# RWKV layer: scores split around the head norms, bonus product on GpSimd, decays and norms set between projections

## The chip, the core and the metric

The program runs on one core of one Trainium2 chip. A core has TensorE (matrix products, PE in the rows), VectorE (DVE), ScalarE (ACT), GpSimd (POOL) and queues of DMAs, each with an instruction stream of its own that is worked off in order; semaphores tie them together. The metric is the time of one execution on the device in microseconds (us), lower being better, given as the median of several runs.

## The reference

The program computes a long stack of layers for 256 tokens of width 1024. The change touches one of them, the RWKV mixer of the second block's layer 1 (16 heads of 64), cut here to what matters:

```python
def rwkv7_mixer(x, mu, w_rkv, w0, w1, w2, a0, a1, a2, g1, g2, k_k, k_a, r_k, ln_g, ln_b, w_out):
    mix = lambda i: x + xx * mu[i]                      # xx: the token before minus this one
    r, k, v = ((mix(i) @ w_rkv[i]).astype(F32) for i in range(3))
    w_log = -jax.nn.softplus(-(w0 + jnp.tanh(mix(3) @ w1) @ w2)) - 0.5
    decay = jnp.exp(-jnp.exp(w_log))
    a = jax.nn.sigmoid(a0 + (mix(4) @ a1) @ a2)
    g = jax.nn.sigmoid(mix(5) @ g1) @ g2
    kk = heads(k * k_k); kk = kk / jnp.maximum(norm_of_head(kk), 1e-12)
    k = k * (1.0 + (a - 1.0) * k_a)
    def step(S, xt):                                    # over the tokens
        r_t, w_t, k_t, v_t, a_t, b_t = xt
        sa = jnp.einsum('bhij,bhj->bhi', S, a_t)
        S = S * w_t[:, :, None, :] + sa[..., :, None] * b_t[..., None, :] + v_t[..., :, None] * k_t[..., None, :]
        return S, jnp.einsum('bhij,bhj->bhi', S, r_t)
    ...
    bonus = (jnp.sum(rh * kh * r_k, axis=-1, keepdims=True) * vh).reshape(B, T, D)
    return ((y + bonus) * g).astype(x.dtype) @ w_out
```

## The kernel before

The kernel does the recurrence in four chunks of 64 tokens. Features lie on the partitions in eight blocks j of 128 (two heads each). A float32 product of the projections is done as three passes of split operands (`hi*hi`, `lo*hi`, `hi*lo`); ScalarE makes `hi`, VectorE makes `lo`. TensorE's order is the order of the code (`manual_schedule`); the other engines' orders come from a scheduler and are fixed when the program is built. What a tile waits for follows from its buffers: a pool tag with n buffers lets the (n+1)-th tile begin only when an earlier one has been read for the last time. PSUM has four banks for products (tag `ps`, two rings of two) and two for accumulators (tag `acc`).

The stages, with the lines of the code before:

- **decays** (L1625 to L1630): for each block two products of 64 rows by 256 columns, `pl2`, and a Sigmoid on ScalarE into `P1`.
- **project** (L1634): a quarter of the key or receptance projection: two accumulations of 24 products into `prk`, each copied by ScalarE into `P2`. The order is key 0, key 1, receptance 0, key 2, receptance 1, key 3, receptance 2, receptance 3.
- **inverse_norms(half)** (L1663): ScalarE squares four key blocks (`kk2`, two buffers of tag `m`, shared with the running sum `cum`), TensorE sums them by head into `pss`, ScalarE takes the root, VectorE the maximum and the reciprocal: `inv`.
- **spread(half)** (L1677): four products of 16 rows spread `inv` over the features: `pk`.
- **phase(j)** (L1688): the running sum of the decays, its exponentials (`E1`, `e3`), the key `km`, the normed key `kk`, the bonus product `f` = receptance * `r_k` * key (L1703, four buffers), and then, in place over `P1` and `P2`, the four decayed operands (L1708 to L1711). L1710 and L1711 overwrite receptance and key of the block. Two `W` buffers (`e4`) serve all phases.
- **turn(j)** (L1716): two products of `f` with the head selector into `pbon` (L1719), and the transposes of block j (L1723), copied by ScalarE into `BKt`.
- **scores(jg)** (L1729): for each of four chunks eight products of 64 rows into two banks `pA`; VectorE masks them into `AM` (L1741), ScalarE copies the diagonal blocks into `Dg` (L1745). `scores(0)` covers the heads of blocks 0 to 3, `scores(1)` those of 4 to 7.
- **the solve** (L1810 to L1839): VectorE transposes `Dg`, does 31 pairs of small steps and transposes back to `Xc` and `Zc`. TensorE meanwhile works on the value projection (`project_v`, four parts) and `products(0)`, then `merge_y` needs `Xc`, `merge_z` needs the copies `Ys`.
- **gates(t, hh)** (L1893): a product into an `acc` bank and five VectorE steps. The recurrence behind it (`middle`, L1929) begins with a product `pU` into the bank that `gates(1, 0)` leaves.

## Time and profile before

| | us |
|---|---|
| median of 3 runs | 2569.16 |
| lowest and highest | 2565.10, 2569.85 |
| the profiled execution, its time | 2571.75 |
| the profiled execution, its span | 2570.0 |
| PE busy | 2448.4 (95%) |
| DVE busy | 1443.1 (56%) |
| ACT busy | 1169.4 (46%) |
| POOL busy | 141.6 (6%) |

The profile is one execution; its time is its span and 1.75 us around it. Times in rows count from the span's start. The RWKV mixer lies between about 1062 and 1280; the change touches 1081 to 1216. A row of the timeline gives the start, the time from the first start to the last end, engine, line, operation, tiles, the count, and in brackets the idle time before it with what ended that. A float32 product shows as two records on PE, a `prk` pass as one.

### The profile page before, as it was taken

The page shows a single profiled execution, that of the slowest core. Times are in us where ns is not written, and L with a number is a line of the kernel's source. Part 1 is how long each engine was busy: PE and PEld are TensorE (multiplying, and loading weights), DVE is VectorE, ACT ScalarE, POOL GpSimd, SP SyncE. Part 2 cuts the span into 40 slices and gives each one's busy share as a digit, 9 for nine tenths or more (in the row PEclk, how much of TensorE's full clock was granted, in tenths as well). Part 3 has the DMA queues.
Part 4 walks back from the last instruction along what each step waited for, and adds up shares of the span by engine and source line. Part 5 has one row for each costly group of instructions (what it writes and reads, how often), then busy time and mean ns, then how long its engine had stood idle before and what let it go on. Part 6 is the DMA issues. An engine that isn't in the chain of part 4 may idle for free.

```text
span 2570.0 us, 42656 instructions
## 1 busy us (share of the span) xinstructions
PE 2448.4 (95%) x17989; PEld 2199.1 (86%) x17989; DVE 1443.1 (56%) x2194; ACT 1169.4 (46%) x1904; POOL 141.6 (6%) x241
## 2 busy tenths in 40 slices
PE   8987679999999999999899999999999999999998
PEld 7764349999899999887799999989999999998998
DVE  7831145558655555588855554565465465477543
ACT  5411134447544544564544444443454454476442
POOL 0100000001200000000000000011100000003000
PEclk9988989999999999999999999999999999999999
DMA  8599996555465565432355565555455555554551
GB/s 280 182 385 419 390 339 212 197 167 177 146 212 181 165 212 180 133 106 90 129 201 179 171 208 182 174 198 166 162 195 183 181 197 181 167 182 164 181 182 64
DMA packets 326016, 502.27 MB, mean 195 GB/s; under 512 B 24833, under 2 KB 278969, under 8 KB 314297
## 3 DMA queue, kind: packets, MB, share of 16 engines
q1 hardware_dynamic: 317616, 481.28, 54.3%
q10 hardware_dynamic: 8200, 18.19, 2.1%
q8 instruction: 143, 2.34, 0.4%
q14 instruction: 57, 0.46, 0.1%
HBM read 498.38 MB, written 1.05 MB: 194 GB/s over the span
## 4 chain that ended last, share of the span: by engine, by line
PE 67%; issue 10%; DVE 6%; ACT 2%; POOL 2%; DMA 2%; ACTq 0%; DVEq 0%; SPq 0%; POOLq 0%
PE gu L362 28%; PE acc L383 18%; PE gut L371 4%; PE pv L371 3%; PE prk L362 2%; PE pu L362 2%; PE pqk L362 2%; PE pg L371 2%; DVE lo L236 1%; PE po L371 1%; DMA wx<-in_w_down_dram 1%; ACT junk L269 1%; POOL rs_r L271 1%; PE pt L304 1%; DVE xn L299 1%
## 5 line engine op out<-in xcount | busy, mean ns | idle before, releaser
L236 DVE TENSOR_TENSOR lo<-raw,hi 128x1024 fp32r<-128x1024 f32 x714 | 851.6, 1217 | 462.1 <-ACT hi L235 462.0
L235 ACT ACTIVATE hi<-raw 128x1024 fp32r<-128x1024 f32 x714 | 723.3, 1045 | 388.1 <-PE acc L383 218.4
L362 PE MATMUL gu<-xh,lo 128*128 128x256 f32 x2304 | 324.0, 284 | 0.0
L362 PE MATMUL gu<-xh,hi 128*128 128x256 f32 x2304 | 323.4, 283 | 0.0
L362 PE MATMUL gu<-xl,hi 128*128 128x256 f32 x2304 | 322.9, 283 | 0.0
L362 PEld LDWEIGHTS gu<-xh,hi 128*128 128x128 f32 x2304 | 300.9, 189 | 5.8
L362 PEld LDWEIGHTS gu<-xl,hi 128*128 128x128 f32 x2304 | 296.7, 189 | 0.0
L362 PEld LDWEIGHTS gu<-xh,lo 128*128 128x128 f32 x2304 | 295.7, 189 | 0.0
L383 PE MATMUL acc<-lo,hh 128*128 128x512 f32 x704 | 224.5, 397 | 0.0
L383 PE MATMUL acc<-hi,hl 128*128 128x512 f32 x704 | 221.6, 394 | 0.0
L383 PE MATMUL acc<-hi,hh 128*128 128x512 f32 x704 | 220.9, 395 | 0.0
L423 ACT ACTIVATE sg<-gu 128x256 f32<-128x256 f32 x144 | 55.3, 384 | 339.8 <-PE gu L362 339.8
L425 DVE TENSOR_TENSOR hm<-sg,gu 128x256 f32<-128x256 f32 x144 | 60.2, 418 | 199.8 <-ACT sg L423 199.8
L383 PEld LDWEIGHTS acc<-lo,hh 128*128 128x128 f32 x704 | 132.8, 189 | 30.6
L383 PEld LDWEIGHTS acc<-hi,hl 128*128 128x128 f32 x704 | 132.2, 188 | 30.2
L383 PEld LDWEIGHTS acc<-hi,hh 128*128 128x128 f32 x704 | 127.2, 188 | 23.7
L270 POOL TENSOR_SCALAR rs_a<-ms 128x1 f32<-128x1 f32 x46 | 19.6, 426 | 1659.3 <-ACT junk L269 1637.9
L1027 PE MATMUL pgu<-wx,xg 128*32 128x256 f32 x816 | 77.9, 430 | 22.5 <-DMA wx<-in_w_gate_dram 14.2
L1027 PEld LDWEIGHTS pgu<-wx,xg 128*32 128x32 f32 x816 | 35.8, 123 | 54.8 <-DMA wx<-in_w_gate_dram 20.2
L236 DVE TENSOR_TENSOR hl<-hm,hh 128x256 fp32r<-128x256 f32 x144 | 60.7, 422 | 35.3 <-ACT hh L235 35.3
L371 PE MATMUL gut<-hi,xh 128*128 128x256 f32 x512 | 78.3, 291 | 0.0
L371 PE MATMUL gut<-lo,xh 128*128 128x256 f32 x512 | 75.1, 287 | 1.6 <-DVE lo L236 1.5
(523 smaller groups left out, 3299.4 us busy)
## 6 DMA issues: line engine op xcount, KB each, us to landing
raw<-in_ffn_w_gu_dram SPq DMA_DIRECT2D x176, 1024.0 KB, 5.1
raw<-in_ffn_w_down_dram SPq DMA_DIRECT2D x88, 1024.0 KB, 4.8
wx<-in_w_gate_dram SPq DMA_DIRECT2D x24, 1024.0 KB, 19.9
wx<-in_w_up_dram SPq DMA_DIRECT2D x24, 1024.0 KB, 19.9
raw<-in_ml_w_in_dram SPq DMA_DIRECT2D x24, 1024.0 KB, 5.2
raw<-in_rt_w_in_dram SPq DMA_DIRECT2D x24, 1024.0 KB, 5.3
wx<-in_w_down_dram SPq DMA_DIRECT2D x22, 1024.0 KB, 11.3
row<-in_norm_g_dram ACTq DMA_DIRECT2D x24, 512.0 KB, 4.2
```

The costliest lines, as they stand in the source:

```text
L235: return (self.nc.scalar.activation(out=hi, in_=src, func=AF.Copy), self.nc.vector.tensor_tensor(out=lo, in0=src, in1=hi.bitcast(F32), op= ...
L236: self.nc.vector.tensor_tensor(out=lo, in0=src, in1=hi.bitcast(F32), op=OP.subtract))
L269: nc.scalar.activation(out=junk[:, qs], in_=src[:, qs], func=AF.Square, scale=mul ** 0.5 / 32.0, accum_out=ms[:, q:q + 1])
L271: nc.gpsimd.tensor_tensor(out=r, in0=a, in1=self.half[:, 0:1], op=OP.pow)
L299: last = nc.vector.scalar_tensor_tensor(out=xn[:, qs], in0=x[:, qs], scalar=rs, in1=g[:, qs], op0=OP.mult, op1=OP.mult)
L304: nc.tensor.transpose(out=pt[:, i, :], in_=xn[:, 128 * k:128 * k + 128], identity=self.c("ident"))
L362: nc.tensor.matmul(out=out, lhsT=a[:, k, c0:c0 + m], rhs=b[:, :, k, :], start=(n == 0), stop=(n == 3 * KD - 1))
L371: nc.tensor.matmul(out=out, lhsT=b[:, t, k, :], rhs=a[:, k, :], start=(n == 0), stop=(n == 3 * KD - 1))
L383: self.down_ins.append(nc.tensor.matmul(out=acc[t][:, n, :], lhsT=s[:, t, :], rhs=r[:, q, 512 * n:512 * n + 512], start=(first and q == 0 ...
L423: nc.scalar.activation(out=sg, in_=gu[:, 0, :], func=AF.Silu)
L425: nc.vector.tensor_tensor(out=hm, in0=sg, in1=gu[:, 1, :], op=OP.mult)
L1027: nc.tensor.matmul(out=p[32 * e:32 * e + 32, 256 * i:256 * i + 256], lhsT=xg[q // 2][:, k, 4 * (q % 2) + e, :], rhs=part(w[e], k, KD), sta ...
```

## The change

1. Of the 16 decays, four stay in front; the other twelve stand one by one behind the passes of `project(xk, kT, 0)` and `project(xk, kT, 1)` (`between`).
2. `inverse_norms(0)` stands inside `project(xr, rT, 0)`, behind its first half.
3. The bonus product is a GpSimd product without `r_k`; `r_k` goes into the selector (`hsr`, one small VectorE product made once).
4. `scores(0)` moves in front of `project(xr, rT, 2)`: chunks 0 and 1 ahead of `inverse_norms(1)`, chunks 2 and 3 behind it; `spread(1)` follows at once, ahead of the projection that stood between. `rwmask` has a buffer of its own.
5. `turn` 0 to 5 stand behind `project(xr, rT, 3)`, ahead of `scores(1)`; 6 and 7 stay behind `project_v(0)`.
6. `project_v(3)` stands whole in front of `merge_y`; behind it come `products(1)`, `merge_z(0)`, `gates(0, 0)`, `merge_z(1)` and the other gates.

```diff
--- before.py
+++ after.py
@@ -1622,20 +1622,32 @@
         P2 = [mp.tile([128, 4, 2, S], F32, name=f"P2{i}", tag=f"P2{i}") for i in range(2)]
         kT = lambda j: P2[j // 4][:, j % 4, 0, :]
         rT = lambda j: P2[j // 4][:, j % 4, 1, :]
-        for j in range(KD):
-            for i, b in enumerate(("w0", "a0")):
-                r = slice(64 * i, 64 * i + 64)
-                p = self.ps.tile([128, S], F32, name="pl2", tag="ps")
-                nc.tensor.matmul(out=p, lhsT=l2[r, 128 * j:128 * j + 128], rhs=hwa[r], start=True, stop=True)
-                nc.scalar.activation(out=P1[:, j, i, :], in_=p, func=AF.Sigmoid, bias=self.col(b, j))
+        def decays():
+            for j in range(KD):
+                for i, b in enumerate(("w0", "a0")):
+                    r = slice(64 * i, 64 * i + 64)
+                    p = self.ps.tile([128, S], F32, name="pl2", tag="ps")
+                    nc.tensor.matmul(out=p, lhsT=l2[r, 128 * j:128 * j + 128], rhs=hwa[r], start=True, stop=True)
+                    nc.scalar.activation(out=P1[:, j, i, :], in_=p, func=AF.Sigmoid, bias=self.col(b, j))
+                    yield
+        decay = decays()
+        for _ in range(4):
+            next(decay)
         xr = self.xt()
         mix_split(0, xr)
-        def project(x, dst, c):
+        def project(x, dst, c, between=None):
             w = self.take()
             for q in range(2):
                 p = self.ps.tile([128, S], F32, name="prk", tag="ps")
-                self.mm_t(p, w, 128 * q, x)
+                for n, (a, b) in enumerate(((w[0], x[0]), (w[1], x[0]), (w[0], x[1]))):
+                    for k in range(KD):
+                        nc.tensor.matmul(out=p, lhsT=a[:, k, 128 * q:128 * q + 128], rhs=b[:, :, k, :],
+                                         start=(n == 0 and k == 0), stop=(n == 2 and k == KD - 1))
+                    if between:
+                        between(3 * q + n)
                 nc.scalar.activation(out=dst(2 * c + q), in_=p, func=AF.Copy)
         self.load_const("headsel", "headsel_t", "segment", "blockodd", pool=mp)
@@ -1646,6 +1658,11 @@
         oka = mp.tile([128, KD], F32, name="oka")
         nc.vector.tensor_scalar(out=oka, in0=ka_t[:, ka0:ka0 + KD], scalar1=-1.0, scalar2=1.0, op0=OP.mult, op1=OP.add)
         WL = mp.tile([128, KD, 4], F32, name="WL")
+        rk_t, rk0 = self.cols["r_k"]
+        hsr = mp.tile([128, KD, 2], F32, name="hsr")
+        nc.vector.tensor_tensor(out=hsr, in0=hs[:, 14:16].unsqueeze(1).to_broadcast([128, KD, 2]),
+                                in1=rk_t[:, rk0:rk0 + KD].unsqueeze(2).to_broadcast([128, KD, 2]), op=OP.mult)
         PU = lambda c: slice(0, 64) if c % 2 else slice(64, 128)
@@ -1700,7 +1717,7 @@
             nc.gpsimd.tensor_copy(out=WL[:, j, :], in_=E1[:, :, 64])
             nc.vector.scalar_tensor_tensor(out=kk, in0=k, scalar=self.col("k_k", j), in1=pk.pop(j), op0=OP.mult, op1=OP.mult)
             nc.vector.tensor_tensor(out=km, in0=km, in1=k, op=OP.mult)
-            nc.vector.scalar_tensor_tensor(out=f, in0=r, scalar=self.col("r_k", j), in1=km, op0=OP.mult, op1=OP.mult)
+            nc.gpsimd.tensor_tensor(out=f, in0=r, in1=km, op=OP.mult)
             nc.vector.scalar_tensor_tensor(out=g, in0=kk, scalar=-1.0, in1=a, op0=OP.mult, op1=OP.mult)
             ar, bk = P1[:, j], P2[j // 4][:, j % 4]
             Ev = E1.rearrange("p (e o) t -> p e o t", o=2)
@@ -1716,7 +1733,7 @@
         def turn(j):
             f = fs.pop(j)
             for t in range(NT):
-                nc.tensor.matmul(out=pb[:, t, 2 * j:2 * j + 2], lhsT=f[:, 128 * t:128 * t + 128], rhs=hs[:, 14:16],
+                nc.tensor.matmul(out=pb[:, t, 2 * j:2 * j + 2], lhsT=f[:, 128 * t:128 * t + 128], rhs=hsr[:, j, :],
                                  start=True, stop=True)
             pt = self.ps.tile([128, 4, 128], F32, name="pbt", tag="ps")
             for c in range(4):
@@ -1726,10 +1743,10 @@
         AM, UV = [], []
-        def scores(jg):
-            for c in range(4):
+        def scores(jg, cs=range(4)):
+            for c in cs:
                 pA = [self.ps.tile([128, 4, 128], F32, name="pA", tag="ps") for _ in range(2)]
                 for i in range(4):
                     for a in range(2):
@@ -1762,10 +1779,9 @@
             for _ in steps:
                 pass
-        project(xk, kT, 0)
-        project(xk, kT, 1)
-        inverse_norms(0)
-        project(xr, rT, 0)
+        project(xk, kT, 0, lambda i: next(decay))
+        project(xk, kT, 1, lambda i: next(decay))
+        project(xr, rT, 0, lambda i: inverse_norms(0) if i == 2 else None)
         spread(0)
         project(xk, kT, 2)
         phase(0)
@@ -1777,33 +1793,32 @@
         for k in range(KD):
             mix(xv[:, k, :], 2, k)
         BKt.extend([big("t1", "BKt", shape=(128, 2, KD, 128)), big("t2", "BKt", shape=(128, 2, KD, 128))])
+        self.load_const("rwmask", pool=mp)
+        rwm = self.c("rwmask")
+        Dg = mp.tile([128, 32, 32], F32, name="Dg")
         project(xk, kT, 3)
+        AM.extend([slot(c % 2, "AM", [128, NH, 128]) for c in range(4)])
+        scores(0, (0, 1))
         inverse_norms(1)
+        scores(0, (2, 3))
         self.ahead = 1
-        project(xr, rT, 2)
         spread(1)
         pb = self.pa.tile([128, NT, 16], F32, name="pbon", tag="acc")
-        turn(0)
-        turn(1)
+        project(xr, rT, 2)
         phase(4)
         phase(5)
         project(xr, rT, 3)
-        turn(2)
-        turn(3)
         phase(6)
         phase(7)
-        self.load_const("rwmask", pool=mp, tag="hwa")
-        rwm = self.c("rwmask")
-        AM.extend([slot(c % 2, "AM", [128, NH, 128]) for c in range(4)])
-        Dg = mp.tile([128, 32, 32], F32, name="Dg")
-        scores(0)
+        for j in range(6):
+            turn(j)
         SV = mp.tile([128, 2, 32, 32], F32, name="SV", tag="P20")
         E = SV[:, 1]
         UV.extend([slot(t, "UV", [128, 2, NH, 64]) for t in range(NT)])
         scores(1)
         every(project_v(0))
-        for j in range(4, 8):
+        for j in range(6, 8):
             turn(j)
         bon = mp.tile([128, NT, 16], F32, name="bon")
         nc.vector.tensor_copy(out=bon, in_=pb)
@@ -1873,16 +1888,13 @@
                     nc.scalar.activation(out=Tt[r, us, 1, :], in_=p[r], func=AF.Copy)
         g2 = self.take()
-        v3 = project_v(3)
-        for _ in range(2): next(v3)
+        every(project_v(3))
         copied = [merge_y(t) for t in range(NT)][0]
         for i in range(2):
             with self.behind([copied]):
                 nc.scalar.activation(out=Tt[:, :, i, :], in_=Zc, func=AF.Copy, scale=bo[:, i:i + 1])
-        for _ in range(3): next(v3)
+        every(products(1))
         merge_z(0)
-        for _ in range(2): next(v3)
-        merge_z(1)
         St = [mp.tile([128, 4, 64], F32, name="St", tag="f", bufs=4) for _ in range(2)]
         SS = big("P21", "SS", shape=(128, NT, D))
         Sd = SS[:, 0, :].rearrange("p (j i) -> p j i", j=KD)
@@ -1903,9 +1915,8 @@
             nc.vector.tensor_tensor(out=s_, in0=p, in1=s_, op=OP.mult)
         gates(0, 0)
-        every(v3)
+        merge_z(1)
         gates(0, 1)
-        every(products(1))
         for hh in range(2):
             gates(1, hh)
```

The DMA queue of SyncE keeps its order row for row, and so does everything ahead of the decays and behind the gates but for two `lo` splits.

GpSimd around phases 4 to 7. Before (`E1` and `WL` are of the phases, `SS` is cleared for the recurrence):

```order
L1700 COPY WL_12047<-E1_12607 128x4 [waits Activation_49]
L1700 COPY WL_12047<-E1_12625 128x4 [waits Activation_49]
L1695 MEMSET E1_12715 128x4 [waits DVE_49,Pool_49]
L1700 COPY WL_12047<-E1_12715 128x4 [waits Activation_49]
L1695 MEMSET E1_12733 128x4 [waits DVE_49,Pool_49]
L1700 COPY WL_12047<-E1_12733 128x4 [waits Activation_49]
L1889 MEMSET SS_13311 128x1024 [waits DVE_49,PE_49,Activation_49]
```

Now (`f` is the bonus product, `P21` holds receptance and key of blocks 4 to 7):

```order
L1712 MEMSET E1_12752 128x4 [waits DVE_49,Pool_49]
L1717 COPY WL_12011<-E1_12752 128x4 [waits Activation_49]
L1712 MEMSET E1_12770 128x4 [waits DVE_49,Pool_49]
L1717 COPY WL_12011<-E1_12770 128x4 [waits Activation_49]
L1720 TENSOR_TENSOR f_12663<-P21_11954,e4_12660 128x256 [waits PE_49]
L1720 TENSOR_TENSOR f_12681<-P21_11954,e4_12678 128x256 [waits PE_49]
L1720 TENSOR_TENSOR f_12753<-P21_11954,e4_12750 128x256 [waits DVE_49,PE_49]
L1720 TENSOR_TENSOR f_12771<-P21_11954,e4_12768 128x256 [waits DVE_49,PE_49]
L1901 MEMSET SS_13322 128x1024 [waits DVE_49,PE_49,Pool_49]
```

Four products were added; those of phases 4 to 7 are last, and each waits for PE.

VectorE in phases 6 (before) and 4 to 6 (now), where the operands are overwritten. Before:

```order
L1708 TENSOR_TENSOR P1_11952<-P21_11954,E1_12715 128x2x2x64 [waits DVE_49,Activation_49]
L1703 SCALAR_TENSOR_TENSOR f_12716<-P21_11954,cols_rw_309,e4_12713 128x256 [waits PE_49]
L1709 TENSOR_TENSOR P1_11952<-e4_12713,E1_12715 128x2x128 [waits Pool_49]
L1710 TENSOR_TENSOR P21_11954<-e4_12713 128x2x2x64 [waits DVE_49]
L1711 TENSOR_TENSOR P21_11954<-e4_12713 128x2x128
L1702 TENSOR_TENSOR e4_12731<-e4_12731,P21_11954 128x256 [waits Activation_49]
L1704 SCALAR_TENSOR_TENSOR e4_12731<-e4_12731,P1_11952 128x256
L1703 SCALAR_TENSOR_TENSOR f_12734<-P21_11954,cols_rw_309,e4_12731 128x256 [waits DVE_49,PE_49,Activation_49]
```

Now:

```order
L1725 TENSOR_TENSOR P1_11952<-P21_11954,E1_12662 128x2x2x64 [waits Activation_49]
L1725 TENSOR_TENSOR P1_11952<-P21_11954,E1_12680 128x2x2x64 [waits Activation_49]
L1727 TENSOR_TENSOR P21_11954<-e4_12660 128x2x2x64 [waits DVE_49,Pool_49]
L1728 TENSOR_TENSOR P21_11954<-e4_12660 128x2x128
L1727 TENSOR_TENSOR P21_11954<-e4_12678 128x2x2x64 [waits DVE_49,Pool_49]
L1728 TENSOR_TENSOR P21_11954<-e4_12678 128x2x128
L1718 SCALAR_TENSOR_TENSOR e4_12750<-P21_11954,cols_rw_309,pk_12602 128x256 [waits DVE_49]
L1718 SCALAR_TENSOR_TENSOR e4_12768<-P21_11954,cols_rw_309,pk_12602 128x256 [waits DVE_49]
```

The bonus product is gone from VectorE; the first overwrite of each block (L1727) now waits for GpSimd.

TensorE from the second half of the norms to the third receptance projection. Before (`pss` sums by head, `pk` spreads):

```order
L1670 MATMUL pss<-kk_12514,c_headsel 16x256
L1670 MATMUL pss<-kk_12517,c_headsel 16x256
L1670 MATMUL pss<-kk_12520,c_headsel 16x256
L1670 MATMUL pss<-kk_12523,c_headsel 16x256
L362 MATMUL prk<-xh,hi 128x256 x8
L362 MATMUL prk<-xh,lo 128x256 x8
L362 MATMUL prk<-xl,hi 128x256 x8
L362 MATMUL prk<-xh,hi 128x256 x8
L362 MATMUL prk<-xh,lo 128x256 x8
L362 MATMUL prk<-xl,hi 128x256 x8
L1682 MATMUL pk<-inv,c_headsel_t 128x256 x4
L1719 MATMUL pbon<-c_headsel,f 128x2 x2
```

Now (`pA` are scores, eight products a chunk):

```order
L1754 MATMUL pA<-P_11952,P_11953 128x128 x16
L1687 MATMUL pss<-kk_12555,c_headsel 16x256
L1687 MATMUL pss<-kk_12558,c_headsel 16x256
L1687 MATMUL pss<-kk_12561,c_headsel 16x256
L1687 MATMUL pss<-kk_12564,c_headsel 16x256
L1754 MATMUL pA<-P_11952,P_11953 128x128 x16
L1699 MATMUL pk<-inv,c_headsel_t 128x256 x4
L1647 MATMUL prk<-xh,hi 128x256 x8
L1647 MATMUL prk<-xh,lo 128x256 x8
```

Two chunks of scores stand on either side of `pss`, and `pk` is no longer behind a projection; the first two turns are gone from here.

ScalarE around the first half of the norms. Before:

```order
L1669 ACTIVATE kk_12176<-P_11953,cols_rw 128x256
L1669 ACTIVATE kk_12179<-P_11953,cols_rw 128x256
L235 ACTIVATE hi<-raw 128x1024
L1671 ACT_TABLE_LOAD
L1671 ACTIVATE inv<-pss 16x256
L1697 ACT_TABLE_LOAD
L1697 ACTIVATE E_12312<-cum 128x4x64
```

Now:

```order
L1651 ACTIVATE P_11953<-prk 128x256
L1686 ACTIVATE kk_12211<-P_11953,cols_rw 128x256
L1686 ACTIVATE kk_12214<-P_11953,cols_rw 128x256
L1714 ACT_TABLE_LOAD
L1714 ACTIVATE E_12314<-cum 128x4x64
L1688 ACT_TABLE_LOAD
L1688 ACTIVATE inv<-pss 16x256
L1651 ACTIVATE P_11953<-prk 128x256
L1715 ACT_TABLE_LOAD
```

An exponential, with its table load, now stands ahead of the root.

## Rows read from the trace of the kernel before

**Rows 1.** Busy time by stretch: window, its length, engines busy (instructions), PEclk, DMA.
```profile
1081.50:1090.30 8.80, 7.51 (x34) 5.49 (x33) 6.13 (x13) 8.58 (x22) 0.00 (x0) 0.81 0.78 266
...
1112.60:1130.00 17.40, 17.40 (x145) 17.26 (x144) 17.32 (x41) 7.83 (x17) 2.65 (x6) 1.00 0.18 62
1130.00:1140.00 10.00, 9.77 (x65) 7.67 (x64) 5.15 (x8) 6.85 (x13) 0.53 (x2) 1.00 0.28 105
1140.00:1144.40 4.40, 4.40 (x26) 4.33 (x26) 4.17 (x12) 2.06 (x7) 0.29 (x2) 0.61 0.12 30
...
1194.90:1198.00 3.10, 3.10 (x128) 3.06 (x128) 2.27 (x2) 1.48 (x3) 0.00 (x0) 0.59 0.94 378
...
1194.70:1215.10 20.40, 19.00 (x352) 14.52 (x352) 15.01 (x23) 10.41 (x16) 0.00 (x0) 0.83 0.30 115
```

**Rows 2.** Timeline of PE, decays to the first spread; columns as told above.
```profile
1084.58 5.76 PE L1629 MATMUL pl<-hwa,raw 64*128 64x256 f32 x24 [0.16 <-ACT P L1630]
...
1101.99 1.04 PE L1670 MATMUL pss<-kk,c_headsel 128*16 128x256 f32 x4
1103.87 1.04 PE L1670 MATMUL pss<-kk,c_headsel 128*16 128x256 f32 x4 [0.85 <-ACT kk L1669]
...
1110.72 1.99 PE L1682 MATMUL pk<-inv,c_headsel_t 16*128 16x256 f32 x8
1112.64 1.21 PE L362 MATMUL prk<-xk,hi 128*128 128x256 f32 x8
```

**Rows 3.** Timeline of ACT: sigmoids of the decays, a table load, copies of scores.
```profile
1084.73 4.19 ACT L1630 ACTIVATE P<-pl,cols_rw 128x256 f32<-128x256 f32 x10
...
1105.18 1.28 ACT L1671 ACT_TABLE_LOAD   x1
...
1154.20 2.34 ACT L1745 ACTIVATE Dg<-pA 32x128 f32<-32x128 f32 x8 [2.54 <-DVE AM L1741]
```

**Rows 4.** Timeline of DVE: reciprocal, phases 6 and 7, masks, first transposition of the solve.
```profile
1107.20 1.74 DVE L1673 RECIPROCAL inv<-inv 16x256 f32<-16x256 f32 x1
...
1149.66 0.48 DVE L1703 SCALAR_TENSOR_TENSOR f<-P,cols_rw,e 128x256 f32<-128x256 f32 x1 [2.34 <-PE pbon L1719]
...
1150.07 0.42 DVE L1709 TENSOR_TENSOR P<-e,E 128x256 f32<-128x256 f32 x1
...
1153.48 2.48 DVE L1741 TENSOR_TENSOR AM<-pA,c_rwmask 128x512 f32<-128x512 f32 x4
...
1162.21 2.48 DVE L1741 TENSOR_TENSOR AM<-pA,c_rwmask 128x512 f32<-128x512 f32 x4 [0.43 <-PE pA L1737]
1165.30 1.96 DVE L1810 STREAM_TRANSPOSE SV<-Dg 128x1024 f32<-128x1024 f32 x1 [0.61 <-ACT Dg L1745]
```

**Rows 5.** Timeline of PE: second spread to the start of the recurrence.
```profile
1140.07 0.61 PE L1719 MATMUL pbon<-c_headsel,f 128*128 128x2 f32 x4
...
1142.61 1.93 PE L362 MATMUL prk<-xh,hi 128*128 128x256 f32 x8
...
1149.12 0.50 PE L1719 MATMUL pbon<-c_headsel,f 128*128 128x2 f32 x4
...
1150.89 2.06 PE L1737 MATMUL pA<-P,P 64*128 64x128 f32 x32
1154.80 8.77 PE L1737 MATMUL pA<-P,P 64*128 64x128 f32 x96 [1.85 <-DVE AM L1741]
1163.53 7.17 PE L1754 MATMUL pv<-raw,xv 128*128 128x256 f32 x32
...
1194.86 3.23 PE L1852 MATMUL pY<-SV,AM 32*32 32x32 f32 x128 [3.05 <-DVE SV L1838]
...
1215.12 1.14 PE L1934 MATMUL pU<-R,Tt 64*64 64x64 f32 x16 [1.27 <-DVE shift L1903]
```

**Rows 6.** GpSimd: a product of 128x256 elsewhere (ns min/median/max), and one copy.
```profile
L1470 POOL TENSOR_TENSOR qk<-ra,rb x16: 728/1226/1758, 1691.2 to 1833.4; 128x256 f32<-128x256 f32 x16
...
1116.56 2.17 POOL L1700 COPY WL<-E 128x4 f32<-128x4 f32 x1 [0.80 <-ACT E L1697]
```

## The prediction

> **What bounds the kernel now.** I read the windows first, then PE's timeline, then, at each gap of PE, the engine that ended it. From 1084 on PE sets the end: the key and receptance projections follow one another, and at 1112.6 to 1130 PE and DVE are both full (17.40 and 17.32 us of 17.40) [rows 1]. The gaps in front of the solve are small: 0.85 us before the second half of `pss`, 1.85 before the second pair of score chunks [rows 2, 5]. From 1165.30 to about 1194.7 the solve on DVE bounds; PE has 28.3 us of cover (1163.53 to 1191.81) and then stands for 3.05 before `pY` [rows 4, 5]. In the tail, 1194.7 to 1215.1, DVE works 15.01 of 20.40 us, and PE waits for DVE at its end [rows 1, 5]. So an edit pays if it takes PE time or a PE wait ahead of 1163, brings the first transposition of the solve (1165.30) forward, or shortens the tail. Four stretches matter: the norms, the phases, the second scores, the tail.
>
> **Decays.** The 24 PE records take 5.76 us, paced by ScalarE (ten sigmoids in 4.19) [rows 2, 3]. Between passes each decay has PE to itself; a small product there costs about what `pk` costs, 1.99 for four, 0.5 each [rows 2]: 12 x 0.5 = 6.0, so +0.2. Bounds: -0.3 by ScalarE's 0.42 a sigmoid, and +1.8 if the lower clock of this stretch (mean 0.81 [rows 1]) falls on the projections instead.
>
> **First norms.** Putting `pss` inside the projection gives the squares a head start, but their two buffers still hold the third and fourth back, so I count half of the 0.85 gap as saved, 0.45. Against that an exponential and its table load now stand ahead of the root on ScalarE. From the last square: load 1.28, exponential 0.42 (the sigmoid's pace), load 1.28, root and maximum 0.74 (what lies between the end of the load at 1106.46 and the reciprocal at 1107.20), reciprocal 1.74 [rows 3, 4]: 5.46, of which about 0.5 runs beside the last products of `pss`, so `inv` comes some 5.0 after them. PE has half a projection for it, 5.81/2 = 2.9 (1104.91 to 1110.72 is a whole one) [rows 2], and waits 2.1 before `pk`. Sum: 2.1 - 0.45 = **+1.6** (+0.4 if the exponential comes in time ahead of the last square, +2.1 without the saving).
>
> The Trainium skill ("ScalarE: Activation LUTs", What ACT_TABLE_LOAD costs) puts a drain of about 1.38 us on top of each load of 1.28. The trace disagrees: the load starts at 1105.18, and the reciprocal behind root and maximum at 1107.20 [rows 3, 4], which leaves 0.74 us for those two and no room for a drain. By the page the two switches would make the wait 2.8 us longer.
>
> **First scores.** Two chunks cost PE 2.06 [rows 5], four 4.1. They keep their waits: before `pss`, 0.4 for a bank (free 1.3 after a mask starts, 1153.48 to 1154.80 [rows 4, 5]); before the fourth chunk, 1.25 for a bank whose copies to `Dg` are queued on ScalarE behind the root and its load (1.28 + 0.4 [rows 3]); before `pk`, 1.0 for the reciprocal, of 1.74 [rows 4]. Taken off a gap of 0.2 that ended there before: **+6.5** together (bounds 4.1 and 8). The turns that stood here go, 1140.07 to 1142.61, -2.5 [rows 5].
>
> **Clock.** Behind `pk` and the turns the granted clock averaged 0.61, a mix of both levels (1.2 and 2.4 GHz), and one pass took 1.93 us [rows 1, 5], where 5.81/6 = 0.97 is a full one: 0.9 lost. This stays for receptance 2, now behind waits and `pk`. The new wait of 2.1 plus `pk` at 1.99 are 4.1 us of little work ahead of key 2; in proportion, 4.1/2.5 x 0.9 = **+1.6** (0 to 2.5).
>
> The end of receptance 3, where turn 2 begins (1149.12 [rows 5]), moves by 0.2 + 1.6 + 6.5 - 2.5 + 1.6 = +7.4, to T = 1156.5.
>
> **Bonus product and its ring.** VectorE saves eight steps of 0.48 [rows 4], but where it is full it only keeps pace with PE, so I count nothing. GpSimd's price is taken as 1.1 us, near the median 1.23 of its product of the same size; the ends are 0.73 and 1.76 [rows 6]. The cost lies in the four buffers of `f`. Those of phases 0 to 3 are read by turns 0 to 3, and these now stand behind receptance 3. So `f` of phase 4 waits for turn 0, and the first overwrite of phase 4 (L1727) waits for it; queued behind it on VectorE are the rest of phases 4 to 7, and the two `W` buffers stay held. VectorE stands for several us. Before, the same ring cost 2.34 (1149.66 <-PE pbon [rows 4]), in phase 6 alone. From T: turn 0's products 0.5, `f` 1.1, two overwrites 0.8; then what took 3.8 before (phase 6's `f` to the first mask, 1149.66 to 1153.48 [rows 4]) with two GpSimd products for two of 0.48, 5.1; handoffs 0.5: T + 8.0 (T + 7 to T + 10 with the ends for three products). Turns at 1.77 for two (1149.12 to 1150.89 [rows 5]) end at T + 5.3, so PE stands about **2.9 us** ahead of `scores(1)`.
>
> GpSimd's copy of four columns took 2.17 us while DVE had no pause [rows 1, 6]. The Trainium skill ("GPSIMD Engine Reference", Specifications) says why: its SBUF ports are shared with VectorE's two-input steps. By that rule the products go nearer the 1.76 end, worth up to +2.0; it is one of the rivals.
>
> **Second scores and solve.** First mask T + 8.4. Before, mask to transposition took 11.82 for eight chunks (1153.48 to 1165.30), two taking 2.91 ((1162.21 - 1153.48)/3) [rows 4]; four take 11.8 - 5.8 = 6.0. Transposition: T + 14.4 = 1170.9, that is **+5.6** (+3.1 without the 1.6 and the 0.9 of the clock). The solve stays 29.4. PE's cover gains six of eight steps of `project_v(3)` (6/8 x 7.17 [rows 5]) and loses two turns: 28.3 + 5.4 - 1.8 = 31.9, from T + 12.6. So PE comes to `pY` at T + 44.5 and `Xc` is there at T + 43.8: the gap of 3.05 is gone, without gain, since DVE set it.
>
> **Tail.** Before, `Xc` to `pU` took 20.4. After: `pY` done 3.2 behind `Xc` (0.7 late, 2.5 for what took 3.23 at clock 0.59 [rows 1, 5]); then VectorE's 15.0 without the second transposition (1.9, as the first [rows 4]), plus two `lo` splits of 1024 columns that now fall in here (1.15 each, a little under two masks of 512, 1.24 [rows 4]): 3.2 + 13.1 + 2.3 = 18.6. **-1.8** (-5.4 if all of DVE's idle went, 0 if another wait takes its place).
>
> **Sum.** +5.6 - 1.8 = +3.8. The profiled execution took 2571.75 (span 2570.0), so 2575.55; it is 2.6 above the median of the three runs, and from the median the forecast is 2569.16 + 3.8 = **2573.0**. A difference under 0.2% (5.1 us) can hardly be told from none here, so this counts as the same.
>
> **Rivals.**
> - *No clock loss.* The projections behind both `pk` run at full clock: 3.8 - 1.6 - 0.9 = +1.3; with GpSimd's product at 0.73 (three of them in the chain, -1.1) +0.2: 2569.4 to 2570.5. For it: key 2 ran at 1.00 behind `pk` before [rows 1]. Against: PE had not stood before that `pk`. 0.10.
> - *Slower: the idle ahead of the second scores takes the clock down.* After 3.05 us of idle the clock was 0.59 before [rows 1, 5]. If 2.9 us do the same, a chunk of scores takes 2.06 on PE (1.03 doubled) against VectorE's pace of 1.46 [rows 4, 5]: 4 x 0.6 = +2.4, and the first value part, at the lower level for its beginning, brings PE 2 us late to `pY`: +8.2, **2577.4**. It decides if the idle is as long as the one in the rows; then the scores, not VectorE, set the transposition. 0.30.
> - *Slower by GpSimd.* Its products go at 1.76 beside VectorE's steps: +2.0, in all +5.8, 2575.0. For it: the copy of 2.17 [rows 6]. Against: VectorE stands while `f` of phase 4 is made. 0.04. (This is the skill's rule on the ports.)
> - *Slower by the loads.* Each table load ahead of the root costs more than its 1.28: `pk` 2.8 later, +6.6, 2575.8. Against it are the 0.74 us behind the load [rows 3, 4]. 0.02. (This is the skill's rule on the drain.)
> - *Faster: the waits are absorbed.* The banks and the reciprocal come in time (-2.6), no clock loss (-2.5), GpSimd at 0.73 (-1.1), another 3.0 of VectorE's idle gone from the tail: 3.8 - 9.2 = -5.4, **2563.8**. For it: VectorE has slack at 1130 to 1140 (5.15 of 10) [rows 1], and 5.4 of idle in the tail. Against: the table loads and the ring stand fixed in the order. 0.12.
>
> **How the numbers follow.** Forecast 0.42, no clock loss 0.10, slower 0.36 in all, faster 0.12; within 0.2% are the first two, 0.52. The forecast's own range is 2569 to 2576. The range asked for goes from 2564.5, which leaves out most of the faster case, to 2580.0, which is the clock's 2577.4 with the GpSimd end (+2.0) and a part of the decays' (+1.6): some 2 in 10 lie outside.
>
> **What would show it.** Right: PE waits about 2 us before `pk` of the first half, 1.2 before the fourth chunk, 1 before `pk` of the second; VectorE stands several us at L1727 of phase 4 until GpSimd's `f` behind turn 0; PE idle near 3 us before `scores(1)`; transposition near 1171; no gap before `pY`; `pU` near 1219. Wrong: VectorE does not stop in phase 4, `scores(1)` follows turn 5 at once, the clock in the first pass of key 2 stays full (or that of the scores falls to half), or the tail is still 20 us.

## The result, and the profile after

The changed kernel takes 2602.12 us in the median of ten runs (2579.51 to 2607.05), the kernel before 2569.73 in the median of ten (2565.10 to 2572.15): a ratio of 1.0112, with a 95% interval of 1.0096 to 1.0128. It is slower by about 32 us. The forecast was +3.8 us, 2573.0, with a range up to 2580.0.

The profiled execution of the changed kernel has a span of 2600.7, 30.7 more than the 2570.0 of before. Its decays began 2.0 us earlier (1079.47 against 1081.47), in a part that the change does not touch, so the mixer itself is 32.7 longer. Counted from the first decay, by four marks that both traces show (the last is the first `pU`):

| stretch | before | after | difference | forecast |
|---|---|---|---|---|
| first decay to the end of the first `pk` | 31.2 | 54.6 | +23.3 | +1.8 |
| from there to the first turn behind receptance 3 (T) | 36.4 | 46.2 | +9.8 | +5.6 |
| T to the first transposition of the solve | 16.2 | 17.5 | +1.3 | -1.8 |
| the transposition to the first `pU` | 49.8 | 48.1 | -1.7 | -1.8 |

The first stretch holds over two thirds of it. The windows of the changed kernel show why (columns as in rows 1: window, its length, PE, PEld, DVE, ACT and POOL busy with instructions, then PEclk, DMA share, GB/s):

```profile
1083.50:1121.60 38.10, 38.10 (x123) 27.61 (x122) 13.21 (x25) 16.61 (x35) 0.00 (x0) 0.50 0.28 90
1123.30:1133.90 10.60, 8.51 (x50) 6.24 (x48) 4.83 (x7) 8.34 (x14) 1.26 (x3) 0.95 0.38 126
1134.00:1137.00 3.00, 3.00 (x17) 3.00 (x17) 2.92 (x9) 1.75 (x3) 1.00 (x3) 0.60 0.00 0
1162.30:1171.30 9.00, 8.96 (x32) 7.74 (x33) 5.13 (x11) 2.99 (x10) 0.19 (x1) 0.50 0.01 2
1190.00:1196.00 6.00, 6.00 (x52) 5.78 (x50) 4.05 (x7) 3.22 (x12) 0.00 (x0) 0.50 0.19 74
```

For 38.1 us PE is busy without a gap, and the granted clock is 0.50 throughout, the lower of its two levels (1.2 GHz). DVE and ACT are mostly idle there: nothing but PE's own pace sets the time. Three shorter stretches at the lower level follow, behind the first `pk`, from the second `pk` on, and in the second scores. PE's timeline shows the long stretch row by row:

```profile
1081.74 0.70 PE L1631 MATMUL pl<-hwa,raw 64*128 64x256 f32 x2 [1.14 <-ACT hg L1616]
1082.58 1.41 PE L1647 MATMUL prk<-xk,hi 128*128 128x256 f32 x8
1083.92 1.22 PE L1631 MATMUL pl<-hwa,raw 64*128 64x256 f32 x2
1085.07 2.08 PE L1647 MATMUL prk<-xk,lo 128*128 128x256 f32 x8
...
1118.60 1.22 PE L1631 MATMUL pl<-hwa,raw 64*128 64x256 f32 x2
1119.75 2.07 PE L1647 MATMUL prk<-xh,hi 128*128 128x256 f32 x8
1121.62 1.91 PE L1647 MATMUL prk<-xh,lo 128*128 128x256 f32 x8
1123.33 1.58 PE L1647 MATMUL prk<-xl,hi 128*128 128x256 f32 x8
```

A decay alone takes 0.70 at the upper level and 1.22 at the lower one, a pass 1.41 where the clock falls within it and 2.08 behind. A decay and a pass together cost 3.15 us there (1083.92 to 1087.07), again and again. Each decay has PE to itself: the pass behind it begins 1.15 us after the decay (1083.92 to 1085.07). As soon as the decays are used up (1119.75) the passes run among themselves, and within three of them the clock is back.

### The profile page after: what moved, and what is told of

The parts are those of the page before. It is cut to its first block, busy times and chain, and to the rows that moved or that the text cites. A ratio compares the mean times of both kernels' runs of the same rounds, so it can differ in the third digit from the quotient of the medians.

```text
span 2600.7 us, 42663 instructions
## 1 busy us (share of the span) xinstructions
PE 2472.4 (95%) x17989; PEld 2213.4 (85%) x17989; DVE 1443.4 (55%) x2187; ACT 1171.9 (45%) x1905; POOL 149.4 (6%) x249
## 4 chain that ended last, share of the span: by engine, by line
PE 67%; issue 10%; DVE 5%; ACT 2%; POOL 2%; DMA 2%; SPq 0%; ACTq 0%; DVEq 0%; POOLq 0%
PE gu L362 28%; PE acc L383 18%; PE gut L371 4%; PE pv L371 3%; PE prk L1647 2%; PE pu L362 2%; PE pqk L362 2%; PE pg L371 2%; PE po L371 1%; DVE lo L236 1%; PE pv L1771 1%; POOL rs_r L271 1%; DMA wx<-in_w_down_dram 1%; ACT junk L269 1%; PE pt L304 1%
## 5 line engine op out<-in xcount | busy, mean ns | idle before, releaser
L270 POOL TENSOR_SCALAR rs_a<-ms 128x1 f32<-128x1 f32 x46 | 19.7, 429 | 1658.2 <-ACT junk L269 1636.8
```

## The experiments

Every kernel was timed beside the kernel before on the same chip, in three groups on three chips; the medians of before were 2568.9 to 2569.3 there, so times of different groups may be compared.

**Decays in front again.** `e1_front` is the changed kernel without part 1:

```diff
-        for _ in range(4):
+        for _ in range(16):
             next(decay)
-        project(xk, kT, 0, lambda i: next(decay))
-        project(xk, kT, 1, lambda i: next(decay))
+        project(xk, kT, 0)
+        project(xk, kT, 1)
```

> The changed kernel with all sixteen decays in front of the key projections again, the other five parts left in. Clock theory (the small products between the passes keep TensorE at 1.2 GHz over both key projections and the first half of receptance 0): key 1 ends near 1102 instead of 1119.75 and the granted clock is 1.00 from 1091 on; of the 31 us some 20 go, so about 2582 (+10 to +13 on the kernel before). Rival (the other parts, table loads, ring of f, first scores, carry the loss and the low clock has another cause): under 8 us go, over 2594.

Measured: 2582.41 (five runs, 2581.80 to 2585.49; ratio 1.0052, 1.0038 to 1.0065). 19.7 us are gone, and the clock is at its upper level when the projections begin (1087.98):

```profile
1081.50:1087.90 6.40, 6.25 (x26) 4.86 (x26) 3.81 (x8) 6.28 (x17) 0.00 (x0) 0.73 0.84 285
1088.00:1102.00 14.00, 14.00 (x118) 14.00 (x118) 10.33 (x18) 11.50 (x23) 0.00 (x0) 1.00 0.65 211
```

It was not the full passes that brought it back. In this run the clock is at 0.50 from 1084.0 and at 1.00 from 1087.3 on, 0.7 us ahead of the first pass. In the kernel before it is the same; PE has nothing but decays until 1090.28 (rows 2):

```profile
1089.00:1089.50 0.50, 0.50 (x4) 0.48 (x2) 0.23 (x1) 0.50 (x3) 0.00 (x0) 0.50 0.87 287
1089.50:1090.00 0.50, 0.50 (x5) 0.29 (x2) 0.46 (x2) 0.50 (x3) 0.00 (x0) 0.86 0.01 2
1090.00:1090.50 0.50, 0.50 (x3) 0.23 (x2) 0.21 (x1) 0.50 (x2) 0.00 (x0) 1.00 0.00 0
```

So a block of 64-row products alone ended the lower level (1086.3 to 1089.7). In such a block neighbouring decays, one on rows 0 to 63 and the next on rows 64 to 127, overlap: twelve take 5.76 us, 0.48 each, more than half of that time at the lower level, where one between two passes takes 1.15.

**Decays alone.** `e2_onlydec` is the kernel before with part 1 of the change only: `project` and `decays` of the changed kernel, four decays in front and twelve one by one between the passes.

> The kernel before with only the twelve decays set between the passes of the first two key projections. Clock theory: the clock stays at 0.50 over both projections, key 1 ends 16 to 20 us later, time about 2587 to 2591. Rival (the low clock needs the other parts): within 3 us of the kernel before.

Measured: 2591.0 in the median of six runs; five lie at 2588.22 to 2593.35, one at 2574.26. Its window 1083.5 to 1121.6 reads PE 37.95 of 38.10 at 0.51. So part 1 alone gives the loss, and in one run of six it mostly did not occur. The changed kernel had the like: two runs of its ten, 2579.51 and 2583.87, lie some 20 us under the rest. Their granted clock over the whole run is 0.981 and 0.977, that of the other eight 0.969 to 0.972 (in `e2_onlydec` 0.978 against 0.973 to 0.976), so they spent less time at the lower level. That it was this stretch in which they did is argued; no such run has a trace.

**What of the decays does it: their rows.** `e3_pad` leaves the order and the number of products and fills each decay up to 128 rows:

```diff
-        hwa = mp.tile([128, S], F32, name="hwa", tag="hwa")
+        hwa = mp.tile([128, 2, S], F32, name="hwa", tag="hwa")
+        nc.gpsimd.memset(hwa[64:128, 0], 0.0)
+        nc.gpsimd.memset(hwa[0:64, 1], 0.0)
...
-                    nc.tensor.matmul(out=p, lhsT=l2[r, 128 * j:128 * j + 128], rhs=hwa[r], start=True, stop=True)
+                    nc.tensor.matmul(out=p, lhsT=l2[:, 128 * j:128 * j + 128], rhs=hwa[:, i], start=True, stop=True)
```

> The changed kernel, decays between the passes, but each decay product uses all 128 rows: the tanh half and the plain half lie in two tiles whose other 64 rows are zero, so products, columns and order are the same. Theory rows (products that fill half of TensorE's rows keep the clock down): the clock returns to 1.00 within key 0, about 2582 to 2585. Rival interruption (any short float32 product between two passes keeps it down, however many rows): 0.50 as before, about 2600.

Measured: 2579.97 (four runs, 2578.37 to 2582.19). The window over both key projections and three rows of PE:

```profile
1083.00:1099.60 16.60, 16.51 (x121) 15.88 (x121) 12.48 (x24) 14.30 (x35) 0.00 (x0) 1.00 0.62 202
```

```profile
1083.09 1.22 PE L1649 MATMUL prk<-xk,hi 128*128 128x256 f32 x8
1084.14 0.60 PE L1633 MATMUL pl<-hwa,raw 128*128 128x256 f32 x2
1084.39 1.30 PE L1649 MATMUL prk<-xk,lo 128*128 128x256 f32 x8
```

With twice the rows, half of them zeros, the clock is at 1.00 from the first decay (1079.88) on, and pass and decay take 1.38 us together (1084.14 to 1085.52) in place of 3.15. Interruption as such does not take the clock down: it is as frequent here. But the clock did not come back here, it never fell; this run cannot say whether it would have come back among such products. And the filling changed two things at once: the decays fill all rows, and the next pass begins 0.25 us behind a decay (1084.14 to 1084.39), where it was 1.15 at the lower level. Which of the two counts is not separated. Shown is that twelve 64-row products, one by one between full passes, give the loss, and that filling them up takes it away.

**Do they pull it down, or only keep it down.** `e4_key1` puts all twelve decays (64 rows) between the passes of key 1, two behind each, and leaves key 0 free of them:

```diff
-        project(xk, kT, 0, lambda i: next(decay))
-        project(xk, kT, 1, lambda i: next(decay))
+        project(xk, kT, 0)
+        project(xk, kT, 1, lambda i: (next(decay), next(decay)))
```

> The changed kernel with the twelve decays all between the passes of key 1, two behind each, none in key 0. If the small products pull the clock down from full: key 0 at 1.00, key 1 at 0.50, some 12 to 14 us over the kernel with the decays in front, about 2594 to 2597. If they only fail to raise a clock that is already low when key 0 begins: key 1 at 1.00 too, within 2 us of the kernel with the decays in front, about 2582.

Measured: 2582.10 (four runs, 2578.01 to 2583.73), as with the decays in front. The windows of key 0 and key 1:

```profile
1082.20:1089.00 6.80, 6.80 (x56) 6.74 (x56) 6.61 (x14) 6.18 (x14) 0.00 (x0) 1.00 0.70 228
1089.00:1099.60 10.60, 10.26 (x66) 7.16 (x64) 5.53 (x11) 8.46 (x21) 0.00 (x0) 1.00 0.58 198
```

The clock holds. PE's rows show that this is not the mix of the changed kernel, though:

```profile
1089.07 0.70 PE L1631 MATMUL pl<-hwa,raw 64*128 64x256 f32 x4
1089.70 1.22 PE L1647 MATMUL prk<-xk,lo 128*128 128x256 f32 x8
1090.85 0.70 PE L1631 MATMUL pl<-hwa,raw 64*128 64x256 f32 x2
```

Two decays (four records) take 0.70 us, as one does: those of a pair run side by side and fill all rows together, in five of the six pairs. In the changed kernel the mix begins right behind four decays and a wait of 1.14 us; the clock falls within the first pass and the mix does not bring it back. Here the same four decays and the same wait stand ahead, then six full passes, and then pairs. Whether the six passes kept the clock up or the pairs did is open; that what came before decides is argued only, from the runs of one kernel that fall 17 to 23 us apart.

**The sixteen rows of `pk`.** `e5_padpk` adds to `e3_pad` that `inv` has 128 rows, zero outside its half, and that `pk` uses them all:

```diff
-        inv = mp.tile([48, S], F32, name="inv", tag="hwa")
+        inv = mp.tile([128, 2, S], F32, name="inv", tag="hwa")
+        nc.gpsimd.memset(inv, 0.0)
...
-                nc.tensor.matmul(out=p[:, i, :], lhsT=hst[q, i, :], rhs=inv[q], start=True, stop=True)
+                nc.tensor.matmul(out=p[:, i, :], lhsT=hst[:, i, :], rhs=inv[:, half], start=True, stop=True)
```

> The changed kernel with the decays filled up to 128 rows and the spread of the norms too: inv has 128 rows, all but the sixteen of its half zero. Theory rows (the 16 rows of pk keep the clock at 1.2 GHz for the passes behind it): both pk at 2.0 us, key 2 and receptance 2 at 1.00 from their first pass, some 6 us under the kernel with only the decays filled up (2580.0), 2572 to 2576. Rival idle (the waits of 1.9 and 1.1 to 1.3 us ahead of pk take the clock down, the rows do not matter): 2580.

Measured: 2575.58 (seven runs, 2573.53 to 2578.62), 4.4 under `e3_pad` (4.0, each against its own kernel before). In `e3_pad` the clock fell at both `pk`, which took 3.12 and 3.78 us; here it stays at 1.00 behind the first (window 1110 to 1120), and around the second it still reads 0.80:

```profile
1110.00:1120.00 10.00, 8.10 (x62) 7.71 (x61) 8.61 (x18) 8.43 (x18) 3.38 (x4) 1.00 0.09 32
1141.60:1150.00 8.40, 8.38 (x50) 7.79 (x51) 5.56 (x12) 3.76 (x12) 0.48 (x3) 0.80 0.01 2
```

In `e10_turns`, below, with the same padding, it was the first `pk` that lost (0.84 over 1105 to 1116) and the second that did not: with gaps of 1 to 2 us in front, the padding does not exclude the fall. That the 4 us come from the rows fits one fall in a profile in place of two; the waits ahead of `pk` as the other part are argued.

**The norms.** `e6_norm` is `e1_front` with the first head norms ahead of receptance 0 again.

```diff
-        project(xr, rT, 0, lambda i: inverse_norms(0) if i == 2 else None)
+        inverse_norms(0)
+        project(xr, rT, 0)
```

> The changed kernel with the decays in front (2582.4) and, besides, the first head norms ahead of receptance 0 again. Theory: the wait of 1.87 us before pk goes, and with it the low clock over key 2 (2.6 us); the gap between the squares comes back (0.6); 2578 to 2579. Rival (the wait only moves, the clock falls anyway): 2582.

Measured: 2578.37 (four runs, 2575.44 to 2580.68), 4.0 under `e1_front`. In its profile the first `pk` begins without a wait (1109.36) and the clock is 1.00 over 1106 to 1120: the wait and the low clock behind it are gone, as expected.

**Scores and turns.** `e7_scores` is `e1_front` with the order from key 3 to `scores(1)` taken from the kernel before, whole (parts 4 and 5 undone).

> The changed kernel with the decays in front and the order from key 3 to the second scores as in the kernel before: scores undivided, turns two by two, rwmask in its old buffer. Norms, GpSimd product, tail stay changed. Theory (the early scores with their three waits, the low clock behind pk, the ring of f): 10 of the 13 us go, 2571 to 2573. Rival (GpSimd product or tail order carry it): 2577 or more.

Measured: 2571.55 (ten runs, 2567.97 to 2577.53; ratio 1.0015, 1.0005 to 1.0025): 10.9 of the remaining 13 us. With the 4.0 of the norms that is more than the 13, so the parts do not simply add up.

**The ring of `f`.** `e10_turns` is `e5_padpk` with four turns moved forward:

```diff
+        turn(0)
+        turn(1)
         project(xr, rT, 2)
         phase(4)
         phase(5)
+        turn(2)
+        turn(3)
         project(xr, rT, 3)
         phase(6)
         phase(7)
-        for j in range(6):
+        for j in range(4, 6):
             turn(j)
```

> The changed kernel with decays and pk filled up to 128 rows (2575.6), and turns 0 and 1 ahead of receptance 2, 2 and 3 ahead of receptance 3, so that the four buffers of f come free before phases 4 to 7 ask for them. Ring theory: the 6.0 us in which VectorE stands at L1727 go, so do the two gaps of 1.0 and 1.3 us of PE in the second scores, the first mask of the second scores comes 1.5 to 3 us earlier: 2572.5 to 2574. Rival (the phases wait for receptance 3 anyway): 2575 to 2576.

Measured: 2571.04 (twelve runs, 2566.50 to 2576.06; ratio 1.0007, 0.9998 to 1.0016), 4.5 under `e5_padpk`, more than expected. The wait of VectorE and the gap of PE in the second scores, first in the changed kernel (POOL, DVE and PE timelines):

```profile
1180.84 1.78 POOL L1720 TENSOR_TENSOR f<-P,e 128x256 f32<-128x256 f32 x2 [4.48 <-PE pbon L1736]
```

```profile
1181.60 0.43 DVE L1727 TENSOR_TENSOR P<-e 128x256 f32<-128x256 f32 x1 [6.00 <-POOL f L1720]
```

```profile
1187.85 0.49 PE L1754 MATMUL pA<-P,P 64*128 64x128 f32 x4 [1.02 <-DVE P L1728]
1189.65 6.53 PE L1754 MATMUL pA<-P,P 64*128 64x128 f32 x52 [1.31 <-DVE P L1728]
```

and in `e10_turns` (DVE and PE):

```profile
1146.35 0.43 DVE L1730 TENSOR_TENSOR P<-e 128x256 f32<-128x256 f32 x1 [0.64 <-POOL E L1715]
```

```profile
1156.66 2.11 PE L1757 MATMUL pA<-P,P 64*128 64x128 f32 x32
1159.23 2.94 PE L1757 MATMUL pA<-P,P 64*128 64x128 f32 x32 [0.46 <-DVE AM L1761]
```

In the changed kernel GpSimd waits for the first turn, VectorE for GpSimd, PE for VectorE. With the turns in time GpSimd no longer waits for PE, VectorE waits 0.64 at most for GpSimd, and the two gaps of PE are gone. Counted from the first decay, the first mask of the second scores comes 3.8 us earlier than in `e5_padpk` (79.9 against 83.7), while the clock lost about as much at one `pk` in either profile.

**The tail alone.** `e8_tail` is the kernel before with part 6 only.

> The kernel before with only the order behind the solve changed: the last value part whole ahead of merge_y, then products, merge_z, gates. The prediction's step: the gap ahead of pY shrinks from 3.05 us to under 1, the idle of VectorE between Xc and pU shrinks, -1.8: 2567.1. Rival (a wait takes its place): 2569 or above.

Measured: 2570.63 (twelve runs, 2564.39 to 2575.29; ratio 1.0003, 0.9994 to 1.0012): the interval runs from 1.5 us faster to 3.1 slower, so the gain of 1.8 lies just outside. The profile shows what stands against it (PE, from `pY` to the start of the recurrence):

```profile
1196.93 2.21 PE L1852 MATMUL pY<-SV,AM 32*32 32x32 f32 x128
...
1211.02 1.12 PE L1893 MATMUL pg<-raw,hg 128*128 128x512 f32 x2 [2.62 <-DVE shift L1900]
1214.92 1.94 PE L1930 MATMUL pU<-R,Tt 64*64 64x64 f32 x16 [2.78 <-DVE shift L1900]
```

`pY` comes without a gap, but 2.1 us later than in rows 5, since the whole last value part stands ahead of it, while turns 4 and 5, which the changed kernel moved forward, are still here; `pU` is as early as before; and behind two waits of 2.6 and 2.8 us the recurrence begins at the lower clock, 1.94 a `pU` where rows 5 have 1.14.

**A version to beat both.** `e9_pads` is the kernel before with the decays between the passes, and decays and `pk` filled up (`e2_onlydec` with the diffs of `e3_pad` and `e5_padpk`); `e11_pads_tail` adds part 6; `e12_pads_again` repeats the first.

> The kernel before with only the decays between the passes, decays and pk filled up to 128 rows. Theory rows: no fall of the clock up to the first scores; a decay then costs 0.25 us between passes against 0.48 in front, so key 1 ends 2 to 3 us earlier, and 0.9 us come back behind the second pk: 2565.5 to 2567. Rival (the clock falls for another reason): 2569 or above, with 0.50 somewhere before 1150.

> The kernel before with decays between the passes, decays and pk filled up to 128 rows, and the changed order behind the solve. If both gains hold: about 2565 to 2567, under both kernels. If the clock falls elsewhere in turn, or the tail gives nothing: 2568 to 2570.

> The kernel before with decays between the passes, decays and pk filled up to 128 rows, once more: its first profile put the mixer 5.2 us ahead of the kernel before, its median gave no gain. If the profile was typical: 1.00 up to 1150 again, and a median of 2564 to 2566. If not: 2568 to 2570, with the clock low somewhere behind the first scores.

Measured: 2568.83 (eleven runs; ratio 1.0005, 0.9995 to 1.0014), 2570.43 (twelve; 1.0004, 0.9994 to 1.0015), 2568.68 (twelve; 0.9995, 0.9987 to 1.0004). None can be told from the kernel before. The windows of the repeat:

```profile
1082.00:1150.00 68.00, 65.77 (x510) 60.17 (x508) 56.02 (x117) 47.57 (x100) 6.61 (x15) 1.00 0.39 130
1150.00:1160.00 10.00, 7.89 (x83) 6.99 (x83) 8.29 (x15) 6.43 (x24) 0.00 (x0) 0.83 0.09 34
1190.00:1200.00 10.00, 7.57 (x140) 6.48 (x140) 8.13 (x10) 4.12 (x6) 0.00 (x0) 0.69 0.51 204
1210.00:1220.00 10.00, 7.37 (x78) 5.94 (x77) 7.87 (x14) 3.12 (x6) 0.00 (x0) 0.71 0.24 93
```

Up to 1150 the clock is full for 68 us, and T comes 3.0 us sooner after the first decay than before, in all three profiles. Of that 2.3 are left at `pY`, and 2.2 at the first `pU`, in this profile; in the first one, 2562.75 us, it was 3.8 at `pU`. Behind that the clock falls at the first scores, where it held before (rows 1 have 0.61 ahead of them instead), and again at `pY` and at the start of the recurrence. That such falls eat the gain in the median is likely and not shown.

## Why the prediction failed, step by step

**Decays: the step that failed.** It took 0.5 us a decay from the `pk` of rows 2, and for the clock a bound of +1.8, by the mean of 0.81 that rows 1 show for that stretch. That mean was read as a price of the place, to be paid once. It was a state: in the kernel before the 64-row products stand in a block and overlap, and the clock is back within that block (1089.7). One by one among twelve passes they did not, for 41 us (1083.4 to 1124.4). Measured: 19.7 us by `e1_front`, 22.1 by `e3_pad`, against +0.2 with bounds from -0.3 to +1.8 (the lower bound is off too: twelve sigmoids at 0.42 would give -0.7). No rival covered it; the slower rival had the lower clock, at another place. Key 0 and key 1 took 37.2 us (1082.58 to 1119.75), and three passes of receptance 0 were still slow, 5.1 us (1119.75 to 1124.85) in place of 2.9. Why this mix did not bring the clock back stays open: half-filled rows, or PE given to one decay for 1.15 us at a time.

It was not the only miss. With the decays in front again 13.1 us are left (`e1_front`), where the rest of the forecast came to 3.6. The clock behind `pk` and the second scores, below, make up most of that.

**First norms: right.** ScalarE's rows are the chain that was summed:

```profile
1125.55 0.94 ACT L1686 ACTIVATE kk<-P,cols_rw 128x256 f32<-128x256 f32 x2 [0.21 <-PE pss L1687]
1126.51 1.28 ACT L1714 ACT_TABLE_LOAD   x1
1127.80 0.42 ACT L1714 ACTIVATE E<-cum 128x256 f32<-128x256 f32 x1
1128.23 1.28 ACT L1688 ACT_TABLE_LOAD   x1
1129.53 0.38 ACT L1688 ACTIVATE inv<-pss 16x256 f32<-16x256 f32 x1
```

`pk` began 4.9 us behind `pss` (forecast 5.0), with a wait of 1.87 (2.1). The gap between the squares fell from 0.85 to 0.23, more than the half that was counted. The root stands 1.30 us behind the start of its load: the drain of 1.38 us that the Trainium skill ("ScalarE: Activation LUTs", What ACT_TABLE_LOAD costs) adds is not seen here either, so the rival of the loads falls.

**First scores: right.** The waits were 0.47, 1.10 and 1.29 us, with 0.17 between the squares (forecast 0.4, 1.25, 1.0):

```profile
1155.37 1.04 PE L1687 MATMUL pss<-kk,c_headsel 128*16 128x256 f32 x4 [0.47 <-DVE AM L1758]
1156.57 1.09 PE L1687 MATMUL pss<-kk,c_headsel 128*16 128x256 f32 x4 [0.17 <-ACT kk L1686]
...
1159.89 1.16 PE L1754 MATMUL pA<-P,P 64*128 64x128 f32 x16 [1.10 <-ACT Dg L1762]
1162.35 3.78 PE L1699 MATMUL pk<-inv,c_headsel_t 16*128 16x256 f32 x8 [1.29 <-DVE inv L1690]
```

**Clock behind `pk`: right in kind, mis-sized.** Taken were 1.6 us for key 2 and 0.9 for receptance 2. Key 2 lost 1.5 in this profile. But the second `pk` took 3.78 in place of 1.99, 1.8 more, and the first four passes of receptance 2 took 6.6 (1166.05 to 1172.66) in place of 4 x 0.97, 2.7 lost and not 0.9. These are 3.6 of the 4.2 that the second stretch of the table has over its forecast.

**Ring and second scores: the mechanism right, the chain 1.8 too short.** VectorE stood 6.00 us at L1727, as described. The first mask came at T + 10.2 (1190.48), not T + 8.4. (The forecast's terms add up to T + 8.0; it goes on with 8.4 and gives no reason.) GpSimd's products were not the reason by themselves: 0.77 in the median of eight, against 1.1 taken. It is VectorE beside them (POOL's and DVE's timelines of the changed kernel):

```profile
1184.84 0.80 POOL L1720 TENSOR_TENSOR f<-P,e 128x256 f32<-128x256 f32 x1 [2.22 <-DVE e L1719]
1186.06 0.78 POOL L1720 TENSOR_TENSOR f<-P,e 128x256 f32<-128x256 f32 x1 [0.42 <-DVE e L1719]
```

```profile
1181.94 0.97 DVE L1728 TENSOR_TENSOR P<-e 128x256 f32<-128x256 f32 x1
...
1184.62 0.41 DVE L1721 SCALAR_TENSOR_TENSOR e<-e,P 128x256 f32<-128x256 f32 x1
1184.95 0.96 DVE L1719 TENSOR_TENSOR e<-e,P 128x256 f32<-128x256 f32 x1
...
1186.17 0.95 DVE L1726 TENSOR_TENSOR P<-e,E 128x256 f32<-128x256 f32 x1
```

A step of VectorE that begins here while a GpSimd product runs ends 0.27 to 0.29 us behind that product's end (1185.91 behind 1185.64, 1187.12 behind 1186.84, 1182.91 behind 1182.62) and takes 0.95 to 0.97 in place of 0.41. Three of them lie in the chain: 3 x 0.55 = 1.6. The two overwrites of phase 5 stand in it as well (1182.83 to 1183.50, 0.7), where two were counted in all, and `f` of phase 4 took 0.72 in place of 1.1: together 1.9 of the 2.2 between T + 8.0 and T + 10.2. The rival "slower by GpSimd" had about the price, 2.0, and the wrong payer. The rule of the Trainium skill that it rested on ("GPSIMD Engine Reference", Specifications: the SBUF interfaces are shared with VectorE) agrees with these rows.

The slower rival of the clock came true in addition, 0.50 over 1190 to 1196: the four chunks took 7.2 us from mask to transposition (1190.48 to 1197.71), not 6.0. Its idle was shorter than thought, 1.02 and 1.31 us in two pieces and not 2.9 in one, since PE could begin the first products: `scores(1)` followed turn 5 at once (1185.62), which the prediction had named as a sign of being wrong.

**Tail: right in the profile.** `Xc` was ready at 1227.21, `pU` began at 1245.80, 18.6 us as forecast, and the gap ahead of `pY` is gone. By itself the part gives no gain that can be measured (`e8_tail`).

**Faster and no clock loss** did not come up: both needed the clock to hold.

## What to carry to other kernels

A low mean clock in a stretch can be a state that something in it ends, and not a fixed price of the place: look for the row at which the clock comes back, and ask whether that row is still there after the change. Before products that fill half of TensorE's rows are set one by one among full ones, ask whether the mixed stretch would still bring the clock back. Where they must stand between, fill them up with zero rows, which took the loss away here; in pairs behind six full passes they did no harm either (`e4_key1`). Moving a product to GpSimd took its time off VectorE, but a step of VectorE that began beside it lost 0.55 us, more than the product had cost there (0.48). And where a ring of buffers is read by steps that are moved back, count its writers: the fifth one waits, with all that is queued behind it.

## What was not expected of the hardware

A PE that was busy for 38.10 of 38.10 us was granted 0.50 throughout. The Trainium skill ("TensorE: Matmul & The Clock Gate", Part 1) has the clock follow how busy the engine has been; here the busy share in the profile alone does not tell it: 38.10 of 38.10 at 0.50 with 64-row products one by one between the passes, 16.51 of 16.60 at 1.00 with the same products at 128 rows. Nor do half-filled rows alone: a block of nothing but 64-row products went from 0.50 to 1.00 (1086.3 to 1089.7 in the kernel before).

In three of sixteen runs of the two kernels with that mix (the changed kernel and `e2_onlydec`) the time was 17 to 23 us shorter than in the rest. A median of few runs of such a kernel can fall on either side.

Zero rows cost nothing here. At full clock a pass takes 0.96 us; with one decay of 128 rows 1.38 (`e3_pad`), with two of 64 rows side by side 1.78 (`e4_key1`, 1092.52 to 1094.30), so 0.42 and 0.41 a decay. A single one of 64 rows between passes at full clock stands in no trace.

GpSimd's product and VectorE's step got in each other's way where both inputs of the step lie in SBUF. In the changed kernel it is five times the short VectorE step that waits for the long product, 0.95 to 0.97 in place of 0.41 to 0.47; two steps that read `pk` from PSUM beside a product were not lengthened (0.48 and 0.47). It can be the other way round: in `e3_pad` a product that began at 1164.30 took 1.80 us, while four VectorE steps in a row kept their 0.41.
